# DeltaNet's v and outputs and attention's v turned by VectorE in 32x32 blocks, placed through DRAM

## The chip, the cores and the metric

The kernel runs on one core of one Trainium2 chip. The metric is the time of one execution on the device, in microseconds (us). The engines named here are TensorE (PE in the profile, with its weight loads as PEld), VectorE (DVE), ScalarE (ACT), GpSimd (POOL) and SyncE (SP). SyncE's queue issues nearly all DMAs; a DMA that has to wait holds up those behind it in that queue.

## The reference

One layer of a decoder trunk on 1024 tokens of width 1024, in float32. One input projection feeds two mixers side by side; a second projection joins them; a gated MLP follows.

```python
h = rmsnorm(x); proj = h @ w_in
# mixer A: gated DeltaNet, 4 heads of 128
qkv = silu(causal_dwconv(proj[:, :1536], 4 taps)); q, k = l2norm(q), l2norm(k)
o_a = gated_delta_rule(q, k, v, g, beta)          # per chunk: a triangular solve, then a state carried over chunks
o_a = rmsnorm(o_a, gdn_norm_w) * silu(z)
# mixer B: attention, 8 heads of 64, branches (128,1), (512,4), (2048,16) merged by their denominators
o_b = dilated_attention(q_b, k_b, v_b)
x = x + concat(o_a, o_b) @ w_out
x = x + (silu(gate) * up) @ w_down                # after rmsnorm and a width-3 depthwise conv
out = rmsnorm(x, final_norm_w)
```

## The kernel before, in words

The activations are held transposed: channels (128 at a time) on the partitions, the 1024 tokens along a row. Every dense product is made of three float32r products of 128x128 by 128x512 (`mm3`): high by high, high by low, low by high parts; `split` makes the two parts, the high one on ScalarE, the low one on VectorE.

`dense` (line 505) walks the 28 column blocks of the input projection in the order of `DENSE`: keys first, then q and v of the four heads alternately, attention's 12 blocks (`a`, four pairs of heads with q, k and v each), then the four gates z. A column is two halves of 24 dense products; VectorE evacuates each half from PSUM, multiplied by the row norm (`xr`, `aqkv`). q, k and v of DeltaNet go through a convolution (`conv_silu`: one ScalarE step, three VectorE steps, SiLU on ScalarE). Attention's blocks are parked in DRAM (`apark`), written in the order of the token classes modulo 4.

What has to have tokens on the partitions is turned. `tokens` (558) makes eight TensorE transposes of 128x128 into PSUM and ScalarE evacuates them. It serves k (`ktok`), the squared norm of q, and v: `vprep` (657) turns v of a head into `vtok`, scaled by the norm `nk`. `finish` (858) turns a head's DeltaNet output back the same way, with the norm's weight `gw2` in the evacuation, and stores it in `mixer`; the z column loads it (`og`), and `gate` (481) multiplies it by silu(z). `att_values` (881) turns v of an attention pair into `vn`, and 16 small DMAs rearrange `vn` into `vc`, the values by class.

Between projection and chain stands the triangular solve: `forward_sub` (663) runs 31 steps on VectorE (`tmp`, `xi`), stores the result (`xdram`, `xtdram`), 24 small DMAs bring it back in blocks, and `merges` (691) joins the blocks by small TensorE products (`x`, `um`, `w`). `chain` (789) then runs the recurrence over eight chunks for all four heads, and `attention` (904) goes pair by pair.

The order of TensorE's list is fixed when the program is built: a planner (`Weave`) replays all streams with its own costs (`Engine`, `product`) and lets the dense columns fill the time in which the chain or attention would wait; each product is stamped with its place. The other engines' lists, SP's among them, are ordered by the scheduler of the framework. Buffers come from rings (`SLOTS`): a tile of the tag `qa`, `ev`, `kt` or `uy` waits for the one so many places earlier.

Of the kernel before, what the change touches and what calls it, by code (L numbers as in the profile page):

```python
# [7 lines left out]
F32 = mybir.dt.float32  # L8
# [7 lines left out]
P = 128  # L16
S = 1024
KT = 8
H = 4
# [125 lines left out]
def hybrid_layer(tc, I, out):  # L145
# [102 lines left out]
    qpark = dp.tile([H, P, S], F32, name="qpark")  # L248
    atpark = dp.tile([H, P, S], F32, name="atpark")
    xpark = dp.tile([KT, P, S], F32, name="xpark")  # L250
    upark = dp.tile([FT, P, S], F32, name="upark")
# [253 lines left out]
    def dense():  # L505

        yield from wv.until("first")
        yield from wv.until("norms")
        wv.add(2, first_keys())

        raw = [raw_weight(I["wi"][0])]
        nxt = wk(None, raw.pop())
        raw.append(raw_weight(I["wi"][1]))
        for i, col in enumerate(DENSE):
            kind, h = col[:2]
            if kind == "z":
                yield from wv.until(("o", h))
            w = nxt
            if i + 1 < len(DENSE):
                nxt = wk(None, raw.pop())  # L520
            if i + 2 < len(DENSE):
                raw.append(raw_weight(I["wi"][i + 2]))
            pair = []
            for hh in range(2):
                pt = bank("hf")
                yield wv.need(pt, *w)
                for k in range(KT):
                    mm3(pt, [t[:, k, :] for t in w], [t[:, half(hh)] for t in xs[k]], k == 0, k == KT - 1)
# [7 lines left out]
                scaled(pair, "xr", kind == "a", t=xr, hs=(hh,))  # L536
            if kind == "k":
                T["k", h] = conv_silu(xr, 4 + h, "kT", "kT*")
                wv.add(3, kprep(h))
            elif kind == "q":  # L540
                q = conv_silu(xr, h, "qT", "qa")
                wv.add(4, qprep(h, q))
            elif kind == "v":
                v = conv_silu(xr, 8 + h, "vT", "qa")
                wv.add(4, vprep(h, v))
            elif kind == "z":
                og = gated[h] = A("og", "kT*")
                sy.dma_start(og, mixer[h])
                if i + 1 < len(DENSE):
                    put_off.append((og, xr))  # L550
                else:
                    gate(og, xr)
            else:
                sy.dma_start(apark[h, col[2]], xr)
                wv.done.add(col)
        wv.done.add("dense")

# [73 lines left out]
    def qprep(h, qT):  # L631
# [22 lines left out]
        d.update(rq=rq, gq=gq)  # L654
        wv.done.add(("q", h))

    def vprep(h, vT):
# [131 lines left out]
    def chain(h):  # L789
# [14 lines left out]
        for c in range(NCH):  # L804
# [7 lines left out]
                qa = qb  # L812
            qT, at = [qa[:, i, (c % 4) * P:(c % 4 + 1) * P] for i in range(2)]
            if c == 0:
                r = vtok[:, cs]
                yield wv.need(ps, vtok, yt)
            else:
                yield wv.need(ps, st, slack=HOP)
                mm(ps[:, 0:P], kT[:, cs], st, 0.215)
                r = tile_(sp, [P, P], F32, "r", "r" + tg, 1)  # L820
                uv.scalar_tensor_tensor(r, ps[:, 0:P], ngam[:, c, h:h + 1], vtok[:, cs], op0=OP.mult, op1=OP.add)
# [18 lines left out]
                mm(po[:, P:2 * P], qT, st, 0.215)  # L840
            mm(po[:, :P], at, w, 0.215)

            ua.activation(vtok[:, cs], po[:, :P], AF.Copy, scale=rq[:, c:c + 1])
            if c:
                uv.scalar_tensor_tensor(vtok[:, cs], po[:, P:2 * P], gq[:, c:c + 1], vtok[:, cs], op0=OP.mult,
                                        op1=OP.add)
            if c < NCH - 1:
                st = sn
            osq = tile_(sp, [P, P], F32, "osq", "osq", 1)
            ua.activation(osq, vtok[:, cs], AF.Square, accum_out=ms[:, c:c + 1])  # L850
# [4 lines left out]
        po_.tensor_tensor(v8(vtok), v8(vtok), ms[:, :, None].to_broadcast([P, NCH, P]), op=OP.mult)  # L855
        wv.add(1, finish(h, vtok))

    def finish(h, osb):
        for hh in range(2):
            pt = yield from next_bank("atr", osb, slack=0.8)  # L860
            for c in range(4):
                i = 4 * hh + c
                tp(pt[:, c * P:(c + 1) * P], osb[:, i * P:(i + 1) * P])
            ot = tile_(sp, [P, 512], F32, "ot", "t2", 2)
            ac.activation(ot, pt, AF.Copy, scale=gw2)
            sy.dma_start(mixer[h][:, half(hh)], ot)
        wv.done.add(("o", h))


# [3 lines left out]
        return t.rearrange("p (n c u) -> p n c u", n=NCH, c=4)  # L873

    def att_load(pi):
        qT, kT, vT = [A(nm, "uy") for nm in ("qT", "kT", "vT")]
        for i, t in ((2, vT), (0, qT), (1, kT)):
            sy.dma_start(t, apark[pi, i])
        return qT, kT, vT

    def att_values(vT):

        vn, vc = A("vn", "kt"), A("vc", "kt")
        for hh in range(2):
            pt = yield from next_bank("atr", vT, slack=ASLACK * (hh == 0))
            for c in range(4):
                i = 4 * hh + c
                tp(pt[:, c * P:(c + 1) * P], vT[:, i * P:(i + 1) * P])
            ac.activation(vn[:, half(hh)], pt, AF.Copy)
        queue = wv.free["sync"]  # L890
        for c in range(4):
            for n in range(4):
                sy.dma_start(vc[32 * n:32 * n + 32].rearrange("u (c b d) -> u c b d", c=4, b=2)[:, c],
                             vn[32 * c:32 * c + 32].rearrange("u (b n d) -> u n b d", b=2, n=4)[:, n])

        wv.ready[vc.tensor.name] = max(wv.pe, wv.ready[vn.tensor.name]) + 6.0
        wv.free["sync"] = max(wv.pe, queue) + 1.6
        return vn, vc

    HALVES = (slice(0, 64), slice(64, 128))  # L900

# [2 lines left out]
    def attention():  # L904
# [7 lines left out]
        qkv = att_load(0)  # L912
        cur = qkv[:2] + (yield from att_values(qkv[2]))

        def scores(pair):

# [118 lines left out]

        pipe = []

        def advance(pair, more=None):
# [3 lines left out]
            if more is not None:  # L1042
                last["values"] = yield from more
            if pair is not None:
                yield from scores(pair)
                pipe.append(pair)
            if done is not None:
                yield from values(done)
                if done[1]["u"] == 3:
                    yield from merge_classes(done[0]["g"])  # L1050
                    give(done[0]["g"])

        for pi in range(4):
            q, k, vn, vc = cur
            for hh in range(2):
                nb = 1 + hh
                if hh == 1 and pi < 3:
                    yield from wv.until(("a", pi + 1, 2))
                    qkv = att_load(pi + 1)
                po = bank("ch")  # L1060
                pb = [A("pb", "qa", shape=(P, 4, 2, P)) for _ in range(nb)]
                po_.memset(pb[-1][:, 2:], 0.0)
# [3 lines left out]
                    wv.done.add("last group")  # L1066
                g = dict(po=po, pb=pb, nb=nb, hh=hh, pi=pi, vc=vc)
                for u in (0, 2):
                    more = att_values(qkv[2]) if (hh, u) == (1, 2) and pi < 3 else None
                    yield from advance([dict(n=4 * hh + i, u=i, q=q, k=k, vn=vn, far=32 * max(4 * hh + i - 1, 0), po=po, pb=pb, g=g)  # L1070
                                        for i in (u, u + 1)], more)
            if pi < 3:
                cur = qkv[:2] + last["values"]
        yield from advance(None)
        wv.done.add("attention")

# [10 lines left out]
    def mixer_splits():  # L1087
# [677 lines left out]
```

## Time and profile before

| | |
|---|---|
| median of 3 runs | 1204.15 us (1203.46 to 1205.03) |
| the profiled execution | 1202.61 us, its span 1200.8 us |
| TensorE busy | 1190.4 us (99%) |
| VectorE busy | 956.5 us (80%) |
| ScalarE busy | 575.3 us (48%) |
| DMA, queue of SyncE | 80896 packets, 151.02 MB, 37.7% of 16 engines |
| granted TensorE clock | 0.998 |

The profile is of one execution. A line of a timeline gives start, duration, engine, line, operation, output and inputs, and in brackets the idle time before it and who ended it. Starts of TensorE's products are closer than their durations, since they are pipelined. Helpers record most instructions, so lines are told apart by tile names: line 191 is every product, 195 every 128x128 transpose, 139 nearly every operation of the other engines.

### The profile page before, as it was taken

To read this page: it belongs to the slowest core of one execution; us is meant where nothing else is said; L and a number is where in the kernel's file an instruction comes from. 1 tells how busy PE (TensorE), PEld (TensorE's weight loads), DVE (VectorE), ACT (ScalarE), POOL (GpSimd) and SP (SyncE) were. 2 spreads that over 40 slices of the span, in tenths; PEclk is the share of its full clock that TensorE was granted. 3 is DMA by queue.
4 is the path that set the end of the run, shared out by engine and by line. 5 is a ranking of instruction groups with operands and counts; after the bars stand their busy time and mean duration, and the time that the engine had idled before them with its cause. 6 is when DMAs were issued, how large, how long until landed. Compare 5 with 4: busy or idle time off the path is not lost.

```text
span 1200.8 us, 18366 instructions
## 1 busy us (share of the span) xinstructions
PE 1190.4 (99%) x7058; PEld 986.1 (82%) x7058; DVE 956.5 (80%) x1532; ACT 575.3 (48%) x1129; POOL 57.1 (5%) x50
## 2 busy tenths in 40 slices
PE   9999999999999999999999999999999999999997
PEld 7888888898777778888888888888888888888887
DVE  7686985483666678767898988989898889898987
ACT  7383344364344445555544544444454454445452
POOL 0212010023000000000000000000000000000001
PEclk9999999999999999999999999999999999999999
DMA  6323234426442313443223222131222395356724
GB/s 237 106 75 102 83 115 129 150 85 238 134 134 84 115 58 124 166 141 122 69 72 106 74 85 102 56 106 53 106 86 72 98 377 217 113 183 218 241 98 157
DMA packets 81704, 152.72 MB, mean 127 GB/s; under 512 B 21552, under 2 KB 32592, under 8 KB 81616
## 3 DMA queue, kind: packets, MB, share of 16 engines
q1 hardware_dynamic: 80896, 151.02, 37.7%
q8 instruction: 55, 0.90, 0.3%
q10 hardware_dynamic: 720, 0.53, 0.1%
q14 instruction: 33, 0.27, 0.1%
HBM read 113.49 MB, written 35.93 MB: 124 GB/s over the span
## 4 chain that ended last, share of the span: by engine, by line
PE 96%; DVE 2%; ACT 1%; DMA 1%; issue 0%; POOL 0%; DVEq 0%; SPq 0%; ACTq 0%; POOLq 0%
PE ps L191 46%; PE pa L191 20%; PE dw L191 17%; PE pc L191 10%; PE ps L195 2%; PE ps L200 1%; DMA wst<-in_wu 0%; ACT sm L141 0%; DVE x1h L139 0%; DMA xt<-in_xT 0%; DVE sm L141 0%; DVE aqkv L139 0%; DVE T L139 0%; DVE wst L139 0%; DVE pair L139 0%
## 5 line engine op out<-in xcount | busy, mean ns | idle before, releaser
L191 PE MATMUL dw<-pr 128*128 128x512 f32 (+1 forms) x984 | 211.4, 376 | 0.0
L191 PEld LDWEIGHTS dw<-pr 128*128 128x128 f32 x984 | 176.7, 188 | 33.6
L191 PE MATMUL ps<-xhi,whi 128*128 128x512 f32 x448 | 184.5, 412 | 0.0
L191 PE MATMUL ps<-xhi,wlo 128*128 128x512 f32 x448 | 175.2, 391 | 0.0
L191 PE MATMUL ps<-xlo,whi 128*128 128x512 f32 x448 | 174.9, 390 | 0.1
L191 PE MATMUL pa<-T,pair 128*128 128x512 f32 x528 | 127.1, 389 | 0.2
L191 PEld LDWEIGHTS pa<-T,pair 128*128 128x128 f32 x528 | 99.0, 188 | 21.2 <-ACT u L139 0.7
L191 PEld LDWEIGHTS ps<-xhi,whi 128*128 128x128 f32 x448 | 84.3, 188 | 19.2 <-issue 3.6
L191 PEld LDWEIGHTS ps<-xhi,wlo 128*128 128x128 f32 x448 | 84.1, 188 | 18.4
L191 PEld LDWEIGHTS ps<-xlo,whi 128*128 128x128 f32 x448 | 84.4, 188 | 14.6 <-DVE xlo L139 0.4
L139 ACT ACTIVATE u<-pa 128x512 f32<-128x512 f32 x44 | 26.3, 598 | 109.7 <-PE pa L191 109.7
L139 DVE SCALAR_TENSOR_TENSOR y<-xu,fcw,y 128x1023 f32<-128x1023 f32 (+1 forms) x44 | 56.3, 1281 | 24.4 <-ACT y L139 24.4
L139 ACT ACTIVATE pr<-wd 128x1024 fp32r<-128x1024 f32 x33 | 35.0, 1061 | 76.1 <-DVE wd L139 39.5
L139 ACT ACTIVATE whi<-wst 128x1024 fp32r<-128x1024 f32 (+2 forms) x38 | 38.5, 1014 | 57.5 <-PE ps L191 48.3
L191 PE MATMUL pa<-B,A 128*128 128x512 f32 x264 | 63.5, 389 | 0.0
L191 PE MATMUL pa<-T,S 128*128 128x512 f32 x264 | 63.4, 389 | 0.0
L191 PE MATMUL pc<-B,pair 128*128 128x512 f32 x264 | 63.4, 389 | 0.0
L191 PE MATMUL pc<-T,S 128*128 128x512 f32 x264 | 63.4, 389 | 0.0
L139 DVE TENSOR_TENSOR wst<-wst 128x512 f32<-128x512 f32 x88 | 60.4, 686 | 0.8
L191 PE MATMUL ps<-B,pair 128*128 128x512 f32 x252 | 60.5, 389 | 0.0
L191 PEld LDWEIGHTS pc<-B,pair 128*128 128x128 f32 x264 | 49.6, 188 | 10.3
L191 PEld LDWEIGHTS pa<-T,S 128*128 128x128 f32 x264 | 49.6, 188 | 10.3
(244 smaller groups left out, 2234.7 us busy)
## 6 DMA issues: line engine op xcount, KB each, us to landing
wst<-in_wu SPq DMA_DIRECT2D x44, 512.0 KB, 3.5
wd<-in_wd SPq DMA_DIRECT2D x44, 512.0 KB, 4.3
wst<-in_wi SPq DMA_DIRECT2D x25, 512.0 KB, 3.6
upark<-y SPq DMA_DIRECT2D x22, 512.0 KB, 3.5
r<-upark SPq DMA_DIRECT2D x22, 512.0 KB, 9.4
apark<-aqkv SPq DMA_DIRECT2D x12, 512.0 KB, 2.8
wa<-in_wd SPq DMA_DIRECT2D x22, 256.0 KB, 2.9
wst<-in_wo SPq DMA_DIRECT2D x8, 512.0 KB, 3.9
```

The source lines that it names most:

```text
L139: return getattr(eng, op)(*a, **kw)
L191: tc.stamp_issue_order_token(nc.tensor.matmul(dst, lhs, rhs, start=start, stop=stop, **kw).ins, TOKEN)
L195: tc.stamp_issue_order_token(nc.tensor.transpose(dst, src, ident).ins, TOKEN)
L200: tc.stamp_issue_order_token(nc.tensor.transpose(dst, src[rows], ident[rows, rows]).ins, TOKEN)
```

## The change

DeltaNet's v: VectorE transposes the 32x32 blocks of a head's v in place of TensorE (`vt`), the result is stored in DRAM (`vdram`) and four DMAs read it back so that tokens are on the partitions (`vtok`); ScalarE scales it per chunk in SBUF. In `vtok` the channels of a chunk now lie in four runs of 32, so the chain reads and writes it through views (`by_chunk`, `by_head`). The outputs: one VectorE block transpose of the whole head (`ft`) and one store; the z column loads it by four DMAs, and z, gate and the split of the gated output use views that keep the order of the blocks (`by_row`, `by_token`). The weight `gw2` moves into the gate. Attention's v: VectorE transposes it when it is evacuated (`avt`), four DMAs write it to DRAM in runs of 32 elements (`avdram`), and `att_load` reads `vn` by four and `vc` by eight DMAs. `vT` of attention, `att_values` and its 16 DMAs are gone. The planner gets a second price for SyncE's small DMAs (`sq_`). None of these tiles passes through TensorE any more.

```diff
+    sq_ = Engine(wv, nc.sync, "sync", 0.05, 0.00036, 2.2)
...
-    apark = dp.tile([4, 3, P, S], F32, name="apark")
+    apark = dp.tile([4, 2, P, S], F32, name="apark")
+    avdram = dp.tile([4, 32, 32, P], F32, name="avdram")
...
+    def by_row(t):
+        return t.rearrange("p (a c i) -> p a c i", a=4, c=NCH)
+
+    def by_token(t):
+        return t.rearrange("p (c a i) -> p a c i", a=4, i=32)
...
-                 ve.tensor_tensor(og, og, y, op=OP.mult)]
+                 ve.scalar_tensor_tensor(og, og, gw2, y, op0=OP.mult, op1=OP.mult)]
...
+                if kind == "z":
+                    ve.tensor_tensor(by_row(xr)[:, :, 4 * hh:4 * hh + 4], by_token(pt), by_token(rstdB[:, half(hh)]), op=OP.mult)
...
-                sy.dma_start(og, mixer[h])
+                for b in range(4):
+                    sq_.dma_start(og[32 * b:32 * b + 32].rearrange("j (a y) -> j a y", a=4),
+                                 mixer[h].rearrange("(a j) (b y) -> b j a y", a=4, b=4)[b])
...
+                    t = A("avt", "ev")
+                    ve.transpose(t.rearrange("p (c n j) -> p n c j", c=4, n=NCH), by_block(xr))
+                    for b in range(4):
+                        sq_.dma_start(avdram[h].rearrange("u x (b j) -> b u x j", b=4)[b],
+                                     t[32 * b:32 * b + 32].rearrange("u (x j) -> u x j", j=32))
...
+    def by_chunk(t, c):
+        return t.rearrange("p (b c j) -> p c b j", b=4, c=NCH)[:, c]
...
-        G[h]["vtok"] = yield from tokens(vT, A("vtok", ("dv", "dw")[h % 2]), G[h]["nk"])
+        vtok = G[h]["vtok"] = A("vtok", ("dv", "dw")[h % 2])
+        t = A("vt", "qa")
+        ve.transpose(t.rearrange("p (a c j) -> p c a j", a=4, c=NCH), vT.rearrange("p (c a i) -> p c a i", c=NCH, a=4))
+        sy.dma_start(vdram[h], t)
+        for a in range(4):
+            sq_.dma_start(vtok[32 * a:32 * a + 32].rearrange("i (b y) -> i b y", b=4),
+                         vdram[h].rearrange("(b i) (a y) -> a i b y", b=4, a=4)[a])
+        for c in range(NCH):
+            ua.activation(by_chunk(vtok, c), by_chunk(vtok, c), AF.Copy, scale=G[h]["nk"][:, c:c + 1])
...
     def finish(h, osb):
-        for hh in range(2):
-            pt = yield from next_bank("atr", osb, slack=0.8)
-            for c in range(4):
-                i = 4 * hh + c
-                tp(pt[:, c * P:(c + 1) * P], osb[:, i * P:(i + 1) * P])
-            ot = tile_(sp, [P, 512], F32, "ot", "t2", 2)
-            ac.activation(ot, pt, AF.Copy, scale=gw2)
-            sy.dma_start(mixer[h][:, half(hh)], ot)
+        yield wv.need(osb, slack=0.8)
+        t = A("ft", "kt")
+        ve.transpose(t, osb)
+        sy.dma_start(mixer[h], t)
...
     def att_load(pi):
-        qT, kT, vT = [A(nm, "uy") for nm in ("qT", "kT", "vT")]
+        qT, kT = [A(nm, "uy") for nm in ("qT", "kT")]
+        vn, vc = A("vn", "kt"), A("vc", "kt")
...
-    def att_values(vT):
...
+        for c in range(4):
+            sq_.dma_start(vn[32 * c:32 * c + 32].rearrange("u (n d) -> u n d", n=NCH),
+                         avdram[pi].rearrange("u (c n) d -> c u n d", c=4)[c])
+        for n in range(4):
+            for b in range(2):
+                sq_.dma_start(vc[32 * n:32 * n + 32].rearrange("u (c b d) -> u c b d", c=4, b=2)[:, :, b],
+                             avdram[pi].rearrange("u (c b n) d -> b n u c d", c=4, b=2)[b, n])
...
-                lo = split(gated[i], *ots[i])
+                g4, hi4, lo4 = by_row(gated[i]), by_token(ots[i][0]), by_token(ots[i][1])
+                ac.activation(hi4, g4, AF.Copy)
+                lo = ve.tensor_tensor(lo4, g4, hi4.bitcast(F32), op=OP.subtract)
```

More of the change, by code (lines that the diff above doesn't have):

```diff
@@ L535, in dense @@
                     xr = A("aqkv" if kind == "a" else "xr", "go" if kind == "k" else "ev")
-                scaled(pair, "xr", kind == "a", t=xr, hs=(hh,))
+                if kind == "z":
+                    ve.tensor_tensor(by_row(xr)[:, :, 4 * hh:4 * hh + 4], by_token(pt), by_token(rstdB[:, half(hh)]), op=OP.mult)
+                else:
+                    scaled(pair, "xr", kind == "a", t=xr, hs=(hh,))
             if kind == "k":
@@ L655, in qprep, with by_head @@
         wv.done.add(("q", h))
+    def by_chunk(t, c):
+        return t.rearrange("p (b c j) -> p c b j", b=4, c=NCH)[:, c]
+    def by_head(t):
+        return t.rearrange("p (b j) -> p b j", b=4)
     def vprep(h, vT):
@@ L814, in chain @@
             if c == 0:
-                r = vtok[:, cs]
+                r = by_chunk(vtok, c)
                 yield wv.need(ps, vtok, yt)
@@ L820, in chain @@
                 r = tile_(sp, [P, P], F32, "r", "r" + tg, 1)
-                uv.scalar_tensor_tensor(r, ps[:, 0:P], ngam[:, c, h:h + 1], vtok[:, cs], op0=OP.mult, op1=OP.add)
+                uv.scalar_tensor_tensor(by_head(r), by_head(ps[:, 0:P]), ngam[:, c, h:h + 1], by_chunk(vtok, c),
+                                        op0=OP.mult, op1=OP.add)
                 yield wv.need(r, slack=HOP)
@@ L841, in chain @@
             mm(po[:, :P], at, w, 0.215)
-            ua.activation(vtok[:, cs], po[:, :P], AF.Copy, scale=rq[:, c:c + 1])
+            oc = by_chunk(vtok, c)
+            ua.activation(oc, by_head(po[:, :P]), AF.Copy, scale=rq[:, c:c + 1])
             if c:
-                uv.scalar_tensor_tensor(vtok[:, cs], po[:, P:2 * P], gq[:, c:c + 1], vtok[:, cs], op0=OP.mult,
-                                        op1=OP.add)
+                uv.scalar_tensor_tensor(oc, by_head(po[:, P:2 * P]), gq[:, c:c + 1], oc, op0=OP.mult, op1=OP.add)
             if c < NCH - 1:
@@ L849, in chain @@
             osq = tile_(sp, [P, P], F32, "osq", "osq", 1)
-            ua.activation(osq, vtok[:, cs], AF.Square, accum_out=ms[:, c:c + 1])
+            ua.activation(by_head(osq), oc, AF.Square, accum_out=ms[:, c:c + 1])
             wv.done.add(("c", h, c))
@@ L875, in att_load @@
     def att_load(pi):
-        qT, kT, vT = [A(nm, "uy") for nm in ("qT", "kT", "vT")]
-        for i, t in ((2, vT), (0, qT), (1, kT)):
+        qT, kT = [A(nm, "uy") for nm in ("qT", "kT")]
+        vn, vc = A("vn", "kt"), A("vc", "kt")
+        for i, t in enumerate((qT, kT)):
             sy.dma_start(t, apark[pi, i])
-        return qT, kT, vT
-    def att_values(vT):
[L883 to L890, printed above, removed]
-        for c in range(4):
[L892 to L898, printed above, removed]
+        for c in range(4):
+            sq_.dma_start(vn[32 * c:32 * c + 32].rearrange("u (n d) -> u n d", n=NCH),
[4 more added lines that the diff above has]
+                             avdram[pi].rearrange("u (c b n) d -> b n u c d", c=4, b=2)[b, n])
+        return qT, kT, vn, vc
     HALVES = (slice(0, 64), slice(64, 128))
@@ L911, in attention @@
         yield from wv.until(("a", 0, 2))
-        qkv = att_load(0)
-        cur = qkv[:2] + (yield from att_values(qkv[2]))
+        cur = att_load(0)
         def scores(pair):
@@ L1036, in attention, with advance @@
         pipe = []
-        def advance(pair, more=None):
+        def advance(pair):
             done = pipe.pop() if pipe else None
@@ L1041, in advance @@
                 yield from turn(done)
-            if more is not None:
-                last["values"] = yield from more
             if pair is not None:
@@ L1058, in attention @@
                     yield from wv.until(("a", pi + 1, 2))
-                    qkv = att_load(pi + 1)
+                    ahead = att_load(pi + 1)
                 po = bank("ch")
@@ L1068, in attention @@
                 for u in (0, 2):
-                    more = att_values(qkv[2]) if (hh, u) == (1, 2) and pi < 3 else None
                     yield from advance([dict(n=4 * hh + i, u=i, q=q, k=k, vn=vn, far=32 * max(4 * hh + i - 1, 0), po=po, pb=pb, g=g)
-                                        for i in (u, u + 1)], more)
+                                        for i in (u, u + 1)])
             if pi < 3:
-                cur = qkv[:2] + last["values"]
+                cur = ahead
         yield from advance(None)
```

8 lines of the change are left out of this document (6 added, 2 removed).

## The prediction, made before the result was known

> **What bounds the kernel now.** I read the page's busy times and its chain of work first, then the table of stretches, then timelines of each engine where the change acts.
>
> ```profile
> PE 1190.4 (99%) x7058; PEld 986.1 (82%) x7058; DVE 956.5 (80%) x1532; ACT 575.3 (48%) x1129; POOL 57.1 (5%) x50
> PE 96%; DVE 2%; ACT 1%; DMA 1%; issue 0%; POOL 0%; DVEq 0%; SPq 0%; ACTq 0%; POOLq 0%
> 150.00:200.00 50.00, 50.00 (x363) 42.34 (x363) 37.97 (x72) 21.48 (x61) 7.24 (x4) 1.00 0.48 140
> 225.00:260.00 35.00, 34.11 (x250) 31.81 (x250) 25.64 (x82) 20.61 (x84) 0.53 (x1) 1.00 0.24 81
> 260.00:300.00 40.00, 39.82 (x238) 34.70 (x237) 17.80 (x45) 18.33 (x58) 16.14 (x11) 1.00 0.62 214
> ```
>
> TensorE is busy for 99% of the span and is 96% of the chain. In the rows of stretches (start, end, length, then busy time of PE, weight loads, DVE, ACT, POOL, granted clock, DMA share, GB/s) it has no hole in 150 to 200 and holes of 0.89 and 0.18 us in the DeltaNet chain of 225 to 300. Dense products of the input projection fill every wait. So each microsecond of work taken from TensorE is a microsecond of span, as long as no new wait opens in its queue, whose order is fixed when the program is built.
>
> **What leaves TensorE.** Twelve sets of eight 128x128 transposes: four of DeltaNet's v, four of attention's v, four of DeltaNet's outputs.
>
> ```profile
> L195 PE MATMUL ps<-ident,vT x64: 270/272/329, 127.3 to 410.2; 128*128 128x128 f32 x64
> L195 PE MATMUL ps<-ident,vtok x32: 272/273/273, 271.1 to 297.5; 128*128 128x128 f32 x32
> 332.92 1.03 PE L195 MATMUL ps<-ident,vT 128*128 128x128 f32 x8
> 333.70 0.48 PE L191 MATMUL ps<-xhi,whi 128*128 128x512 f32 x1
> 334.02 0.40 PE L191 MATMUL ps<-xlo,whi 128*128 128x512 f32 x1
> 334.25 0.39 PE L191 MATMUL ps<-xhi,wlo 128*128 128x512 f32 x1
> 271.11 0.60 PE L195 MATMUL ps<-ident,vtok 128*128 128x128 f32 x4
> 271.47 0.48 PE L191 MATMUL ps<-xhi,whi 128*128 128x512 f32 x1
> 271.78 0.39 PE L191 MATMUL ps<-xlo,whi 128*128 128x512 f32 x1
> ```
>
> Their 272 ns overlap, so the price is read from starts. Dense products start 0.23 apart (334.02 to 334.25). Eight transposes hold the queue from 332.92 to 333.70, and the product behind them keeps it 0.32 instead of 0.23: 0.78 + 0.09 = 0.87. Four take 0.36 + 0.08 = 0.44. In the old TensorE list nine groups have eight and six have four (outputs in the chain): 9 x 0.87 + 6 x 0.44 = 10.5 us. Floor without the switching penalty: 9 x 0.78 + 6 x 0.36 = 9.2.
>
> **What VectorE gets.** Twelve 128x1024 block transposes. The trace shows none. The nearest rows are the strided copy of 128x1024 below (1.13) and, as upper end, two halves of the strided move into aqkv (2 x 1.10 = 2.2); I take 1.15, nearest to the copy, since both read SBUF. [...] Twelve by 1.15 is 14 us of an engine that is 50 to 75% busy in these stretches, so the sum hardly matters; what matters is whom each of them delays.
>
> **The first stretch, 120 to 200.** Here VectorE is nearly full, because the forward substitution (tmp and xi, 31 steps) runs between the evacuations, and the merges on TensorE wait for its result, through DRAM.
>
> ```profile
> L139 DVE TENSOR_TENSOR aqkv<-ps,rstdB 128x512 f32<-128x512 f32 x24 | 26.5, 1103 | 26.9 <-PE ps L191 26.8
> 127.69 1.22 DVE L139 TENSOR_TENSOR wlo<-wst,whi 128x1024 fp32r<-128x1024 f32 x1
> 173.46 0.18 DVE L139 TENSOR_TENSOR xi<-xi,tmp 128x31 f32<-128x31 f32 x1
> 173.67 1.13 DVE L139 COPY mt<-xi 128x1024 f32<-128x1024 f32 x1
> 177.60 0.69 DVE L139 TENSOR_TENSOR xr<-ps,rstdB 128x512 f32<-128x512 f32 x1 [2.80 <-PE ps L191]
> 179.61 3.91 DVE L139 SCALAR_TENSOR_TENSOR qT<-xr,gcw,qT 128x1023 f32<-128x1023 f32 x3
> 173.71 0.32 SPq L139 DMA_DIRECT2D xdram<-xi  x1
> 184.04 1.99 SPq L139 DMA_DIRECT2D x<-xdram  x4
> 186.07 3.94 SPq L139 DMA_DIRECT2D um<-xtdram  x8
> um<-xtdram SPq DMA_DIRECT2D x16, 32.0 KB, 2.0
> 198.13 2.21 PE L191 MATMUL ps<-x,um 32*32 32x32 f32 x128
> 192.82 1.05 PE L191 MATMUL ps<-qT,kT 128*128 128x128 f32 x8
> 193.63 0.48 PE L191 MATMUL ps<-xhi,whi 128*128 128x512 f32 x1
> 193.95 0.40 PE L191 MATMUL ps<-xlo,whi 128*128 128x512 f32 x1
> ```
>
> Before: the last xi ends at 173.6, xi is stored at 173.71, the last of 24 small loads is issued by 190.0 and lands 2.0 later, at 192.0; the merges start at 198.13. Slack 6.1. After, in the new VectorE list, three transposes stand between the steps, and the last xi step has fallen behind the third convolution of head 3's q. Its second evacuation waits for TensorE (177.60), which now comes two v groups earlier, at 175.9. The convolution then ends at 183.5 - 1.7 = 181.8, plus four short steps of about 0.1 wedged between: xi is done at 182.2, stored 8.5 later than before. If every transpose took 2.2 instead, three of them would put off xi by at most 3.2 more. The small loads follow in the same chain: 192.0 + 8.5 = 200.5. Ahead of the second store SP now also passes the parking of head 3's q, done at about 183 like the copy mt, so that costs nothing more.
>
> TensorE arrives earlier: its list has nine more dense products ahead of the merges (9 x 0.23 = 2.0) but not three v groups (2.6), nor head 3's q transposes (0.87) and its two qT,kT groups (0.81 + 0.09 each, 1.8). 198.1 + 2.0 - 5.3 = 194.8. The merges of heads 0 and 1 find their data: their twelve loads went out before 184.04, landed by 186.0, and with 8.5 added that is 194.5. Those of heads 2 and 3 would start at 195.9 and wait until 198.5 to 200.5 for the last eight loads: **a new stall of 3.5 to 4.5, I take 3.9**. It is paid once: behind it the list goes on with work that is ready (the w copies have 18 dense products of cover, 4.1 us, against copies of about 0.7).
>
> **The v round trip.** vtok is now stored to DRAM and read back before ScalarE scales it, and ScalarE's list has these eight scalings between the first step and the SiLU of the next head's q, as before. What is queued behind them is that SiLU, which TensorE waits for.
>
> ```profile
> 128.60 2.15 ACT L141 ACTIVATE vtok<-ps,nk 128x128 f32<-128x128 f32 x8
> 147.78 0.60 DVE L139 SCALAR_TENSOR_TENSOR at<-ps,bp,dec 128x128 f32<-128x128 f32 x2
> 133.45 1.06 ACT L139 ACTIVATE qT<-qT 128x1024 f32<-128x1024 f32 x1 [2.71 <-DVE qT L139]
> 138.43 1.03 PE L195 MATMUL ps<-ident,qT 128*128 128x128 f32 x8
> qpark<-qT SPq DMA_DIRECT2D x4, 512.0 KB, 2.7
> x<-xdram SPq DMA_DIRECT2D x8, 64.0 KB, 2.3
> qat<-qpark SPq DMA_DIRECT2D x8, 256.0 KB, 3.2
> r<-upark SPq DMA_DIRECT2D x22, 512.0 KB, 9.4
> ```
>
> Head 0: transpose at 127.7, done 128.9; store landed at 131.7; four loads at about 0.48 (1.99 for four x<-xdram) issued by 133.5, landing 2.3 to 3.2 later, 136.3 in the middle; scaled at 138.4; SiLU done at 139.5. TensorE comes to that q at 138.43 - 0.87 + six dense products (1.4) = 138.9. **Stall 0.6** (0 to 1). Head 1's transpose stands among its at products (147.78), done near 149, and the same 10.6 to the SiLU make 159.6; TensorE's next q group comes two columns on, 96 x 0.23 + one q and two qT,kT groups 2.7 = 24.5 later, at 163.4: 3.8 of slack. Head 2's, 172 + 10.6, ends with the convolution of head 3's q and delays its parking by nothing beyond the 183 above. Head 3's comes behind the merges; transposed at an estimated 220 and scaled 9 later, at 229, it stands ahead of one w copy, and the chain's first w product is due at about 233 (225.5, two groups of three, 27 dense products).
>
> **The rest.** In the chain seven block transposes of 1.15 (one v, two attention v, four outputs) get into VectorE's list beside the recurrence. There such a block cost before:
>
> ```profile
> 238.46 1.05 DVE aqkv L139
> ```
>
> It stands in the chain of waits, and all blocks of this size together (some nine) left TensorE 0.89 + 0.18 us idle; seven more cost 0 to 1.5, I take 0.8. Strided views in runs of 32 elements I cost at nothing (aqkv's 1.10 is for runs of one). SP's queue: 64 vc issues, 8 output stores, 4 og loads, 4 v stores and 4 v loads of attention go; 20 for DeltaNet's v, 48 placement loads, 16 og pieces, 16 avdram pieces and 4 output stores come; none feeds TensorE within 10 us except as above, and the column weights are loaded a column or more ahead. At the end the gated outputs are split in pieces and 15 dense products less stand between attention and the output projection:
>
> ```profile
> 469.07 0.69 DVE L139 TENSOR_TENSOR xr<-ps,rstdB 128x512 f32<-128x512 f32 x1 [0.40 <-PE ps L191]
> 474.73 1.23 DVE L139 TENSOR_TENSOR olo<-og,ohi 128x1024 fp32r<-128x1024 f32 x1 [1.13 <-ACT ohi L139]
> 471.26 80.55 PE ps L191 x354
> ```
>
> Head 3's low part is ready at 476.0 and asked for after 36 products, 471.3 + 8.2 = 479.5; 3.5 of slack cover the 1.9 or so that the new order costs. Nothing changes from there on.
>
> **Sum.** -10.5 + 3.9 + 0.6 + 0.8 = -5.2 on the span of 1200.8 and the profiled 1202.6: 1197.4. That execution is 1.5 below the median of the runs (1204.15), so the same saving gives 1199.0 there; I predict **1198.5** between the two. A measurement tells a change of about 0.2% (2.4 us).
>
> **Rivals.**
> 1. *The merges do not wait* (the DRAM loads are quicker on a quieter queue, or VectorE ends the substitution early). For it: DMA has 1% of the chain of work so far; against it the 8.5 us by which xi is late, against 6.1 of slack. Saving 10.5 - 1.0 = 9.5: 1194.5. Chance 0.17.
> 2. *The stall also costs clock.* If TensorE stands for 4 us and the 18 dense products behind the merges then run at half rate, that is 18 x 0.23 = 4.1 more; taking half of it, 1200.5. For it: this would be the longest hole since the start; against: the granted clock is 1.00 in every stretch above, and no hole of this size is in the trace to judge by. Chance 0.13. [...]
> 3. *Slower: ScalarE's queue stands behind the DRAM round trip.* If the store and loads of vtok take L longer than the 7.5 us reckoned (rows of 9.4 for one load exist, in a crowded queue), head 0's q group is late by L in full, and head 2's by L less about 1 delays head 3's SiLU, its parking, and behind it in SP's queue the second store and the merges. The loss is about 2 L - 1; it eats the 5.2 and 2.4 more at L = 4.3, so 1207 at L = 4.5. For it: four waits in an in-order engine; against: medians of 2 to 4 us for all DMAs in this stretch. Chance 0.13, with 0.07 for a smaller L that ends within 0.2%.
> 4. The forecast, a stall of 3 to 5 at the merges: 0.50, its own range 1196 to 1201.
>
> The range leaves out a round trip at its worst and the full saving with quick loads: 1193 to 1204.5. Faster: 0.50 + 0.17 + 0.13 less a little for stalls that add up = 0.77; same 0.08; slower 0.15.
>
> **What would show it.** Right: no L195 transposes of vT or vtok; StreamTranspose rows of 1.1 to 1.3; xdram stored at about 182; a hole of about 4 us in TensorE at 196 to 200 inside the x,um products, then the chain's first vtok,um product at about the old time (225.5), and the up-projection 5 to 6 us earlier. Wrong: that hole missing, or holes of microseconds at the qT transposes near 139 and 163, or in the chain at the w products; transposes over 2.2; a clock under 1.00 behind the hole.

## The result and the profile after

The changed kernel takes 1207.05 us (median of 20 runs; 1204.27 to 1211.55), the kernel before 1203.07 (20 runs; 1202.29 to 1205.29): 1.0032 times as long, 95% interval 1.0025 to 1.0040. It is slower by about 4 us; forecast were 5.6 us less (1204.15 to 1198.5). The profiled execution has a span of 1204.3, 3.5 more than before.

The page of after, busy times and the chain by engine:

```profile
PE 1186.3 (99%) x6962; PEld 979.8 (81%) x6962; DVE 970.7 (81%) x1544; ACT 568.0 (47%) x1113; POOL 52.5 (4%) x50
PE 89%; DVE 3%; DMA 3%; ACT 1%; SPq 1%; issue 1%; POOL 0%; DVEq 0%; ACTq 0%; POOLq 0%
```

The 96 products have gone (7058 to 6962), but TensorE's busy time fell by 4.1 us only, and its share of the chain from 96% to 89%: DMA, VectorE and SP's queue now set its pace in places. What TensorE waits for in after, summed (waited for: us, times, longest); these are the rows that are new or larger than in the kernel before, which has 0.5 for w and none of the other three:

```profile
PE ps L192 <- ACT w L141: 4.4, 2, 3.9
PE ps L201 <- DVE sm L141: 1.5, 2, 1.0
PE ps L196 <- ACT qT L139: 1.2, 1, 1.2
PE ps L192 <- ACT pb L141: 1.0, 1, 1.0
```

The table of stretches of after (columns as in the prediction):

```profile
150.00:200.00 50.00, 49.86 (x350) 41.63 (x349) 40.80 (x73) 20.81 (x46) 3.58 (x3) 1.00 0.53 156
225.00:260.00 35.00, 30.45 (x191) 27.09 (x190) 20.10 (x59) 17.93 (x66) 0.00 (x0) 0.95 0.44 144
350.00:400.00 50.00, 48.94 (x547) 37.38 (x545) 36.16 (x109) 18.68 (x68) 2.23 (x5) 1.00 0.40 117
555.00:600.00 45.00, 44.74 (x202) 36.86 (x201) 35.28 (x48) 22.98 (x33) 1.95 (x1) 0.96 0.27 93
```

The hole forecast at the merges is not in 150 to 200 (0.14 us). There is one of 4 us in 225 to 260, where none was forecast, and the granted clock is 0.95 there and 0.96 in 555 to 600, where it was 1.00 before. The chain of waits of after (`...` marks rows left out, here and below) shows what leads up to the hole:

```profile
216.58 1.16 DVE vt L139
217.76 3.76 DMA vdram<-vt
...
223.21 5.05 DMA vtok<-vdram
...
228.59 2.14 ACT vtok L141 x7
...
230.94 4.25 PE ps L192 x12
```

It is head 3's v: transposed by 217.7, stored, read back by 228.3, scaled on ScalarE. The product at which TensorE stops does not read that v. But look at ScalarE's list (timeline of ScalarE, then of TensorE, in after; w is ScalarE's copy of one part of a PSUM tile, and the wke,ktok product writes another part of the same tile; one such product is two records, as the 28 of the fourth experiment are 56):

```profile
225.15 0.54 ACT L141 ACTIVATE w<-ps 128x128 f32<-128x128 f32 x2 [2.53 <-DVE wke L141]
228.28 2.45 ACT L141 ACTIVATE vtok<-vtok,nk 128x128 f32<-128x128 f32 x8 [2.60 <-DMA vtok<-vdram]
230.63 0.26 ACT L141 ACTIVATE w<-ps 128x128 f32<-128x128 f32 x1
226.40 0.61 PE L192 MATMUL ps<-wke,ktok 128*128 128x128 f32 x4
230.94 0.80 PE L192 MATMUL ps<-wke,ktok 128*128 128x128 f32 x2 [3.94 <-ACT w L141]
```

Three heads start the recurrence at the same time. ScalarE copies two of the three w; then come head 3's eight scalings, which wait for DRAM; the third w copy, which could have followed at 225.7, stands behind them. TensorE's third wke,ktok product waits for that copy, 3.94 us.

### The profile page after: what moved, and what is told of

Read it like the earlier page. It is cut to its first block, busy times and chain, and to the rows that moved or that the text cites. A ratio compares the mean times of both kernels' runs of the same rounds, so it can differ in the third digit from the quotient of the medians.

```text
span 1204.3 us, 18192 instructions
## 1 busy us (share of the span) xinstructions
PE 1186.3 (99%) x6962; PEld 979.8 (81%) x6962; DVE 970.7 (81%) x1544; ACT 568.0 (47%) x1113; POOL 52.5 (4%) x50
## 4 chain that ended last, share of the span: by engine, by line
PE 89%; DVE 3%; DMA 3%; ACT 1%; SPq 1%; issue 1%; POOL 0%; DVEq 0%; ACTq 0%; POOLq 0%
PE ps L192 40%; PE pa L192 20%; PE dw L192 17%; PE pc L192 10%; SPq L139 1%; PE ps L201 1%; PE ps L196 1%; DMA vtok<-vdram 1%; DMA vdram<-vt 1%; DMA wst<-in_wu 0%; DVE wlo L139 0%; ACT vtok L141 0%; PE warm L192 0%; DVE x1h L139 0%; DMA wst<-in_wi 0%
## 5 line engine op out<-in xcount | busy, mean ns | idle before, releaser
L192 PEld LDWEIGHTS pc<-T,S 128*128 128x128 f32 x264 | 49.5, 188 | 10.3
```

The lines of the kernel that those rows point to most:

```text
L192: tc.stamp_issue_order_token(nc.tensor.matmul(dst, lhs, rhs, start=start, stop=stop, **kw).ins, TOKEN)
```

## Experiments

Two theories. **A**: the loss is ScalarE's in-order list: what stands behind the DRAM round trip of vtok is late, and the idle TensorE then loses clock too (0.95 in 225 to 260). **B**: the loss is elsewhere (attention's small waits, VectorE's extra blocks), and the w copy only came last. All times below are medians, with the ratio to the kernel before (1203.3 in these comparisons); the ratio is taken over all runs and can differ a little from that of the medians.

**1. The scaling on GpSimd.**

```
-        for c in range(NCH):
-            ua.activation(by_chunk(vtok, c), by_chunk(vtok, c), AF.Copy, scale=G[h]["nk"][:, c:c + 1])
+        vt = vtok.rearrange("p (b c j) -> p b c j", b=4, c=NCH)
+        po_.tensor_tensor(vt, vt, G[h]["nk"][:, None, :, None].to_broadcast([P, 4, NCH, 32]), op=OP.mult)
```

> The change with one edit: the scaling of vtok by nk is one GpSimd product per head instead of eight ScalarE copies, so nothing on ScalarE stands behind the DRAM round trip any more. Theory A (ScalarE's queue behind the round trip is what turned the saving into a loss): the wait of 3.9 us for w near 231, the 1.2 us at head 0's q near 140 and the clock of 0.95 in 225 to 260 all go; 1.2 + 3.9 + 1.7 of half-rate time = 6.8 us, so about 1200.2 against 1207.05, and under the kernel before. Theory B (the loss is spread over the attention's waits and a slower clock there; the wait for w only names who came last, and the first chain product would wait for vtok itself instead): within 2 us of 1207.

Measured: 1197.37 us, ratio 0.9946 (0.9934 to 0.9958), 9.7 us under the change and 5.9 under the kernel before. What TensorE waits for in this kernel, and the stretch of the hole:

```profile
PE ps L192 <- ACT w L141: 1.5, 2, 1.0
225.00:260.00 35.00, 33.94 (x239) 31.17 (x238) 25.71 (x77) 20.24 (x78) 2.83 (x2) 1.00 0.43 141
```

The waits for q and for w near 231 are gone and the clock is 1.00. That is A's direction, but 2.9 us more than A's price: this edit also changes the planner's view, and TensorE's list came out different. So the second experiment changes the order on ScalarE and nothing else, and the third keeps at least TensorE's list.

**2. Only the order on ScalarE.** Head 3's scalings are put behind the three w copies, by an ordering edge without any new wait between engines; TensorE's, VectorE's, SP's and GpSimd's lists are those of the change.

```
+            inst = ua.activation(w, ps[:, P:2 * P], AF.Copy)
+            for one in G[3]["scaled"] if c == 0 and h < 3 else ():
+                after(one, inst, "the first chunks go first")
...
```

> The change with ScalarE's list altered in one place: head 3's eight scalings stand behind the w copies of heads 0, 1 and 2 instead of between the second and the third. TensorE's, VectorE's, SP's and GpSimd's lists are those of the change. Theory A (the order on ScalarE, not the transfers): the wait of 3.9 us near 231 and the 1.7 us of half-rate behind it go, the 1.2 us at head 0's q stays: 1207.05 - 5.6 = about 1201.4. Theory C (GpSimd's version gained by its other TensorE list): within 1.5 us of 1207.

Measured: 1200.92, ratio 0.9978 (0.9967 to 0.9988). ScalarE's timeline in this kernel and its stretch:

```profile
225.86 0.85 ACT L141 ACTIVATE w<-ps 128x128 f32<-128x128 f32 x3 [2.54 <-DVE wke L141]
228.96 2.45 ACT L141 ACTIVATE vtok<-vtok,nk 128x128 f32<-128x128 f32 x8 [2.25 <-DMA vtok<-vdram]
225.00:260.00 35.00, 33.93 (x233) 30.87 (x233) 24.88 (x74) 21.80 (x83) 0.52 (x1) 1.00 0.52 163
```

The round trip is as long as before (the scalings begin at 228.96 instead of 228.28), and TensorE no longer waits for it at this place. One copy, 0.3 us of work, moved past eight others is worth 6.1 us (5.6 expected). In the traces the two kernels differ by this one move: the instructions of TensorE, VectorE, GpSimd and SP come in the same order. That rules out the theory that only another TensorE list had gained, and leaves B nothing of this wait.

**3. The same for heads 0 to 2**, on top of the second: their scalings now stand behind the SiLU of the next head's q.

```
+            for one in G[j - 1].get("scaled", ()) if 1 <= j <= 3 else ():
+                after(one, T["silu", j], "the next queries go first")
...
```

> As w_first, and the scalings of heads 0, 1 and 2 stand behind the SiLU of the next head's q as well. Theory A: the 1.2 us at head 0's q go too: 1207.05 - 6.8 = about 1200.2. Theory C: within 1.5 us of 1207.

Measured: 1200.07, ratio 0.9970 (0.9960 to 0.9981), as A has it. The step from the second kernel, 0.85 us, is not settled by the times, since the intervals overlap; the wait of 1.2 us for head 0's q is gone from the trace. TensorE's list is that of the change, but VectorE's and SP's came out a little different between 141 and 176 us. The first products of the up-projection in TensorE's timelines before, in the change and here:

```profile
556.62 2.88 PE L191 MATMUL pa<-B,A 128*128 128x512 f32 x12
558.60 2.88 PE L192 MATMUL pa<-B,A 128*128 128x512 f32 x12
551.68 2.88 PE L192 MATMUL pa<-B,A 128*128 128x512 f32 x12
```

From the change to here 6.9 us of waits and clock went, 6.8 expected.

**4. The clock.** 28 products whose result is overwritten, just ahead of the product that waits for w.

```
+                if (h, c) == (2, 0):
+                    early = bank("atr")
+                    for _ in range(28):
+                        ... nc.tensor.matmul(early[:, :P], ktok[:, cs], kT[:, cs], start=True, stop=True) ...
```

> The change with 28 products of 128x128 whose result is overwritten, on TensorE just ahead of the product that waits for w (about 3 us of work inside the wait of 3.9 us); all else as in the change. If the idle stretch is what halves the clock afterwards: granted clock 1.00 in 225 to 260 instead of 0.95, and about 1.7 us less, 1205.4. If the clock falls for another reason (a power or memory event at that place): 0.95 again and 1207.

Measured: 1207.62, ratio 1.0033 (1.0020 to 1.0045). Rows of the filled kernel, the first from TensorE's timeline, the others from the table of stretches:

```profile
229.12 6.42 PE L870 MATMUL ps<-kT,ktok 128*128 128x128 f32 x56
199.00:203.00 4.00, 4.00 (x33) 3.18 (x27) 0.70 (x1) 0.59 (x1) 0.00 (x0) 0.57 0.59 95
225.00:260.00 35.00, 34.55 (x243) 31.72 (x240) 18.21 (x52) 16.52 (x60) 0.00 (x0) 1.00 0.45 147
```

The time decides nothing: the products took 6.4 us, not 3, so 2.5 more than the wait they filled; and this profile lost clock at another place (199 to 203, behind a wait of 0.75 us inside the merges). The clock does: with TensorE kept busy it stays at 1.00 where it fell to 0.95. The three profiles with this wait left as it is (the change, and the two kernels of the sixth experiment that keep DeltaNet's v on VectorE) all show 0.95. So the idle stretch is what halves it there (0.50 in 232 to 234 of the change, last section), and not something else at that place; for the filled kernel this rests on one profile.

**5. A longer trip.** vtok is read back twice.

```
-        for a in range(4):
-            sq_.dma_start(vtok[32 * a:32 * a + 32]...)
+        for _ in range(2):
+            for a in range(4):
+                sq_.dma_start(vtok[32 * a:32 * a + 32]...)
```

> The change with vtok read back twice (the same four loads again, behind the first four), so DeltaNet's v waits some 4 to 5 us longer for DRAM. The scheduler, which reckons with the longer trip, now puts head 0's and 1's SiLU and all three w copies ahead of the scalings on ScalarE. Theory A (only what stands behind the trip in ScalarE's list counts): the waits go although the trip is longer: 1200 to 1202.5. Theory D (the length of the DRAM trip is on the path): two trips of 4 to 5 us more, 1212 or above.

Measured: 1215.06, ratio 1.0088 (1.0074 to 1.0101). A's number missed by some 13 us, and D's (1212 or above) was met. The traces show why, and it is A's mechanism at places that the expectation left out. The first w copies and two SiLU did come first; head 2's scalings still stand ahead of the SiLU of head 3's q, and head 3's ahead of the next chunk's w copies. ScalarE's, SP's and TensorE's timelines of this kernel:

```profile
190.91 2.45 ACT L141 ACTIVATE vtok<-vtok,nk 128x128 f32<-128x128 f32 x8 [7.76 <-DMA vtok<-vdram]
193.26 1.04 ACT L139 ACTIVATE qT<-qT 128x1024 f32<-128x1024 f32 x1
194.33 0.32 SPq L139 DMA_DIRECT2D qpark<-qT  x1
202.58 1.99 SPq L139 DMA_DIRECT2D x<-xdram  x4
204.94 0.28 PE L192 MATMUL ps<-x,um 32*32 32x32 f32 x2 [4.73 <-DMA x<-xdram]
...
249.76 0.80 PE L192 MATMUL ps<-wke,ktok 128*128 128x128 f32 x2 [2.48 <-ACT w L141]
```

The scalings wait 7.8 us for DRAM, the SiLU behind them is late, so is the parking of that q in SP's list, and the 24 small loads behind it: the merges wait 6.0 us, and 5.1 us of clock go with them. At 249.8 TensorE waits another 2.5 us for a w copy, with 1.7 of clock. This is the path of the prediction's third rival (head 2's scalings, head 3's q and its parking, the merges), and the hole that the forecast had put into the change itself. There it has not opened, but its margin is gone: waits of 0.5 to 0.75 us for x<-xdram stand at this place in the second, the fourth and two later kernels (no_out, pool_dv_out). So theory D is right in this much: at this length the trip is on the path, through the list of ScalarE. TensorE's and VectorE's lists differ from the change's here too, so the time alone does not divide the loss between order and length.

**6. One part undone.** Three kernels, each with one part of the change taken back to its form before (the lines are those of no_dv; in the other two the 0 stands for AV or OUT). In the last of them GpSimd writes the outputs in plain order, so that TensorE can turn them.

```
+    DV, AV, OUT = 0, 1, 1
...
+        if not DV:
+            yield from tokens(vT, vtok, G[h]["nk"])
...
```

> The change without its first part: DeltaNet's v goes through TensorE and ScalarE again, attention's v and the outputs stay with VectorE. Theory A: four groups of eight transposes come back (4 x 0.87 = +3.5 us), the two waits and the half-rate stretch go (-6.8): about 1203.8. Theory B: nothing of the loss sat there, so +3.5: about 1210.5.

> The change without its second part: attention's v is turned on TensorE again, with its 64 small moves. Four groups come back (+3.5). Theory A: the small waits at the turns of the pairs (0.6 + 1.0 + 0.8 + 1.0 us in the trace of after) are what this part costs, and they go: about 1207, no gain and no loss. Theory B: attention's v on VectorE and SP's queue is where the loss sits, with the clock behind it (half rate from 571 on, 1.6 us): 1203 to 1205.

> The change without its third part: DeltaNet's outputs go back through TensorE and ScalarE (the GpSimd product writes them in plain order first). One group of eight and six of four come back (+3.5). Theory A: the outputs cost nothing of the loss, so about 1210.5. Theory B, in the form that VectorE's extra blocks in the chain (ft, the strided gate and split) feed the waits: 1205 to 1207.

Measured: 1201.56, 1214.75 and 1207.94, ratios 0.9987 (0.9978 to 0.9996), 1.0092 (1.0077 to 1.0106) and 1.0038 (1.0024 to 1.0051). The first fits A with 2.2 us to spare. The second misses every expectation: with attention's v back on TensorE the change gets 7.7 us slower instead of staying where it was. TensorE's timeline at the end of its attention:

```profile
469.97 0.72 PE L201 MATMUL ps<-ident,sm 64*128 64x64 f32 x16 [0.75 <-DVE sm L141]
...
474.30 0.66 PE L192 MATMUL ps<-pt,vn 128*64 128x128 f32 x8 [1.24 <-DVE pt L141]
481.03 0.50 PE L192 MATMUL ps<-ohi,whi 128*128 128x512 f32 x1 [2.47 <-DVE oT L139]
```

Its list has no dense product of the input projection left behind the attention; the kernel before has 39 and the change 24. The planner had spent them earlier as cover. The third lies between the two theories' numbers: outputs on VectorE are worth 0.9 us here by the medians, not 3.5, and the two intervals overlap.

**7. Single parts with the GpSimd scaling**, to see what a part is worth once the round trip is out of ScalarE's way (the edits of 1 and 6 together; the last turns attention's v in two halves):

```
-                    ve.transpose(t.rearrange("p (c n j) -> p n c j", c=4, n=NCH), by_block(xr))
+                    for o in range(0, NCH, 4):
+                        ve.transpose(t.rearrange("p (c n j) -> p n c j", c=4, n=NCH)[:, o:o + 4], by_block(xr)[:, o:o + 4])
```

> Only the first part of the change, with the scaling on GpSimd: DeltaNet's v by VectorE and DRAM; attention's v and the outputs go through TensorE as before. Theory P (the parts add up; what a part is worth is its transposes): four groups of eight go, 32 transposes at the 0.1 us that they take in a row plus their switches, 3.4 us: about 1199.9. Theory Q (a part's worth hangs on how the fixed order spends the dense products; 21 are left behind the attention here, 39 in the kernel before): waits of 1 to 3 us at the end of the attention, 1201 to 1203.

> The change with the GpSimd scaling, but attention's v on TensorE. Six dense products are left behind the attention (42 with attention's v on VectorE). Theory P: 1197.4 + 3.4 = 1200.8. Theory Q: the last softmax and the last splits have no cover, 3 to 5 us of waits near 460 to 480 on top: 1204 to 1206.

> The change with the GpSimd scaling, but DeltaNet's outputs through TensorE. 48 dense products are left behind the attention. Theory P: 1197.4 + 3.4 = 1200.8. Theory Q: no waits at the end of the attention and fewer VectorE blocks in the chain, so part of the 3.4 comes back: 1198.5 to 1200.

> The change with the GpSimd scaling and attention's v turned in two halves of 128x512, the first as soon as its half is evacuated, so that no block of 1.25 us stands between the second evacuation and the softmax's copies. If these blocks cause the small waits in the attention (0.9 us here, 3.3 us in the change): 0.5 to 1 us less, 1196.6. If not: 1197.4 as without.

Beside the medians: the dense products left behind the attention in TensorE's list, and TensorE's waits between 440 and 500 in the profile.

| On VectorE | us | ratio, 95% interval | left | waits 440 to 500 |
|---|---|---|---|---|
| nothing (before) | 1203.3 | 1 | 39 | 0 |
| DeltaNet's v | 1204.43 | 1.0009 (1.0000 to 1.0018) | 21 | 2.0 |
| DeltaNet's v, outputs | 1204.11 | 1.0006 (0.9997 to 1.0015) | 6 | 2.0 |
| DeltaNet's v, attention's v | 1198.17 | 0.9958 (0.9945 to 0.9970) | 48 | 0 |
| attention's v, outputs (no_dv) | 1201.56 | 0.9987 (0.9978 to 0.9996) | 48 | 0 |
| all three | 1197.37 | 0.9946 (0.9934 to 0.9958) | 42 | 0 |
| all three, v in halves | 1195.54 | 0.9943 (0.9929 to 0.9957) | 42 | 0 |
| the change (ScalarE scales) | 1207.05 | 1.0032 (1.0025 to 1.0040) | 24 | 1.0 |
| the change without the outputs | 1207.94 | 1.0038 (1.0024 to 1.0051) | 41 | 0 |
| the change without attention's v | 1214.75 | 1.0092 (1.0077 to 1.0106) | 0 | 5.8 |

Theory P does not hold: the parts do not add up. Theory Q has the direction each time, but the sizes only partly: 1204.43 lies above its 1201 to 1203 and 1198.17 just under its 1198.5 to 1200. DeltaNet's v alone takes four groups off TensorE and gains nothing: by the medians it ends 1.1 us later than before, and its interval begins at 1.0000. Its trace has one wait at the last softmax and lost clock behind it, together 3.7 us, about what the transposes saved (TensorE's timeline of that kernel; the dense products behind the wait start 0.43 apart instead of 0.23):

```profile
460.74 0.73 PE L201 MATMUL ps<-ident,sm 64*128 64x64 f32 x16 [2.00 <-DVE sm L141]
...
461.81 0.63 PE L192 MATMUL ps<-xlo,whi 128*128 128x512 f32 x1
462.24 0.63 PE L192 MATMUL ps<-xhi,wlo 128*128 128x512 f32 x1
```

Attention's v is worth 6 to 8 us in these lists (1204.43 to 1198.17, 1204.11 to 1197.37, 1214.75 to 1207.05), twice its transposes. In the kernels of the table the waits at the end go with the products left there: none with 39 or more, 1.0 with 24, 2.0 with 21 and 6, 5.8 with none. That the number left is the cause was not tried by itself, with all else held. The halves gain 1.8 us by the medians, more than the 0.5 to 1 expected, but 0.4 by the ratios, and the two intervals overlap: that gain is not settled. This last kernel is the fastest found: 7.8 us under the kernel before by the medians, 6.9 by the ratio.

## Why the prediction was wrong, step by step

- **What bounds.** Right: TensorE does. Fewer transposes were worth time wherever no new wait took it.
- **What leaves TensorE, -10.5.** A little too much: summed from start to start in TensorE's timelines, the transposes took 6.4 (vT) and 3.1 (vtok), 9.5 in all. With three switches less between the dense runs it is 9.8 at most, nearer to the floor of 9.2. Error 0.7.
- **What VectorE gets, 1.15 each.** Good: 1.24 in the trace of after.

```profile
L139 DVE STREAM_TRANSPOSE ft<-vtok x4: 1223/1240/1246, 274.7 to 308.5; 128x1024 f32<-128x1024 f32 x4
```

- **The merges, a new stall of 3.9.** Wrong: 0.4 at most. The substitution did end late as forecast; the rows (SP's timeline and TensorE's, after):

```profile
183.41 0.34 SPq L139 DMA_DIRECT2D xdram<-xi  x1
193.41 2.88 SPq L139 DMA_DIRECT2D x<-xdram  x4
196.32 3.95 SPq L139 DMA_DIRECT2D um<-xtdram  x8
196.12 2.59 PE L192 MATMUL ps<-x,um 32*32 32x32 f32 x128
```

  The failed step is "wait until 198.5 to 200.5 for the last eight loads". The x,um products need the x of heads 2 and 3, landed at 197.5 by the chain of waits, and not the um loads issued behind them; and TensorE came at 196.1, not 194.8. The size was not worked out cleanly either: a start at 195.9 and data at 198.5 to 200.5 make 2.6 to 4.6, not 3.5 to 4.5. The margin at this place is used up, as the fifth experiment shows.
- **The v round trip, 0.6 at head 0, none later.** This is the step that decided. Head 0 cost 1.2. For head 3 the text says that vtok "stands ahead of one w copy, and the chain's first w product is due at about 233". The copy was seen; who waits for it was not. It is not only the product that reads w, but already the wke,ktok product into the same PSUM tile, due at 227.0, some 6 us before the 233 that the forecast reckoned with. The trace of before had shown this wait in a row of TensorE's timeline that I did not read for it:

```profile
257.51 0.49 PE L191 MATMUL ps<-wke,ktok 128*128 128x128 f32 x2 [0.47 <-ACT w L141]
```

  The trip was also longer than the 7.5 us reckoned, 10.5 for head 3 (217.7 to 228.3) against 7.7 for head 0; the second experiment shows that the length did not matter once the order was right. Cost: 3.9, and 1.7 of clock.
- **The chain and the rest, 0.8 and nothing.** The recurrence kept its two waits of 0.5, as before: 0. The attention did not: 0.56 and 0.96 for the softmax and 0.99 for pb are marked waits, and one group of score products took 1.63 instead of 0.85: 3.3. The third experiment's kernel, whose VectorE list is that of the change from 176 us on, shows what stands in front at one such place (VectorE's timeline there):

```profile
379.35 1.11 DVE L139 TENSOR_TENSOR aqkv<-ps,rstdB 128x512 f32<-128x512 f32 x1 [0.52 <-PE ps L192]
380.50 1.25 DVE L139 STREAM_TRANSPOSE avt<-aqkv 128x1024 f32<-128x1024 f32 x1
381.66 0.72 DVE L141 COPY pt<-ps 128x256 f32<-128x256 f32 x2
```

  The new transposition sits between an evacuation and the copies that TensorE waits for through ScalarE's pb. I had priced these blocks in the recurrence and not in the attention. The kernel of the first experiment has the same blocks and another TensorE list, and no wait for pb; so this cause is read from the trace and not isolated.
- **"Nothing changes from there on."** Wrong by 1.7 in this execution: half rate from 572 on (last section).
- **Sum.** -9.8 + 0.4 + 1.2 + 3.9 + 1.7 + 3.3 + 1.7 = +2.4, against +3.5 measured in the span. Of the rest, 0.8 is in the group of score products at the marked wait for pb, which takes 2.66 from start to start instead of 0.85 with only 0.99 marked, and 0.4 at the very start, where the 20 warming products end 0.42 later; behind the last product the span is 0.2 shorter. That makes +3.4.
- **Rivals.** The third had the mechanism (ScalarE behind the DRAM round trip), its direction and even its 1207, with a chance of 0.13, but at heads 0 and 2 and by the length of the trip; it came at head 3 and by the order, so that its 1207 agrees is luck. The first had it right that the merges do not wait, but not why (neither quicker loads nor an earlier substitution: the products read less than was reckoned), and its 1194.5 leaves out the waits elsewhere. The second (the stall costs clock) came true on top of the third, where the two had been given as separate cases. That the products behind such a stall run at half rate was an assumption of the forecast; the trace of after shows it at this place: from 230.7 to 234.1 us, 3.4 us, dense products start 0.43 apart instead of 0.23, and 1.7 us are lost.
- With the order mended (third experiment) the first product of the up-projection starts 4.9 us earlier than before, against a forecast of 5.2. That closeness is luck: errors of both signs cancel in it, no stall at the merges, but waits in the attention.

## What to carry to other kernels

When data takes a detour through DRAM, the question is not only whether it is back in time for its reader, but which instruction stands behind that reader in its engine's in-order list, and who waits for that one; a wait can sit at a product that only shares the PSUM tile (3.94 us here). Put such a reader on an engine with a nearly empty list (GpSimd here, busy for 4% of the span), or order it behind what is ready: one copy moved was worth 6 us. And where a fixed order hides waits under filler work, gains need not add up: here the waits went with where the filler was left over, so count it behind the last stage first.

## What the runs showed of the hardware

In these profiles clock was lost in portions. In stretches of 1 us, every drop of the granted clock between 20 us and the last few us of the span, in the fourteen profiles, took about 1.7 us or a multiple (1.67 to 1.71, in after 1.71 and 1.70; 5.12 once, in the fifth experiment). In after both portions are half rate for 3.4 us, from 230.7 to 234.1 and from 572.0 to 575.4. The first begins in the hole at the w product, 0.2 us before TensorE goes on at 230.94. The table of stretches of after shows that drop:

```profile
228.00:230.00 2.00, 0.00 (x0) 0.00 (x0) 0.00 (x0) 1.72 (x6) 0.00 (x0) 1.00 0.95 318
230.00:232.00 2.00, 1.06 (x4) 0.96 (x5) 0.22 (x2) 1.84 (x5) 0.00 (x0) 0.68 0.92 323
232.00:234.00 2.00, 2.00 (x6) 1.61 (x5) 1.20 (x2) 0.00 (x0) 0.00 (x0) 0.50 0.99 393
234.00:236.00 2.00, 2.00 (x10) 1.57 (x10) 0.00 (x0) 0.00 (x0) 0.00 (x0) 0.97 0.85 229
```

The second portion came without such a hole; the marked wait in front of it is 0.26 us. At the start of the up-projection TensorE runs 16 products one column wide and then waits for a ScalarE result, or not. Rows of TensorE's timeline, before and then after:

```profile
566.83 1.84 PE L191 MATMUL ps<-ones,rstdB 128*128 128x1 f32 x16
568.80 3.02 PE L191 MATMUL pa<-T,pair 128*128 128x512 f32 x12
568.81 1.84 PE L192 MATMUL ps<-ones,rstdB 128*128 128x1 f32 x16
570.91 4.56 PE L192 MATMUL pa<-T,pair 128*128 128x512 f32 x12 [0.26 <-ACT u L139]
```

Where this stretch took 1.70 to 1.97 us (eleven profiles) the next twelve products took 2.8 to 2.9; where it took 2.05, 2.10 and 2.24, they took 4.4. So 0.1 us more of waiting went with 1.7 us of clock (1.97 in before, 2.10 in after). Fourteen single profiles do not show whether the length of this stretch decides it; a kernel that varies this length alone was not run.

The same TensorE list lost its portions at different places: at 230.7 and 572.0 in the change, at 388.1 in the second kernel, at 565.2 in the third. The runs of the change spread over 7.3 us, those before over 3.0, and the granted clock on record for each run goes with it: 0.996 in the two fastest (1204.27 and 1204.72), 0.993 and 0.992 in the two slowest (1211.03 and 1211.55). A thousandth of this span is 1.2 us, so the clock makes up most of that spread.
